# A hybrid decoder layer on one core: the low halves of weights kept in DRAM between two token halves, and new rates for gathered steps

## The chip, the cores and the metric

The kernel runs on one core of a Trainium2 chip. The metric is the device time of one execution in microseconds (us). Before the change it was 3117.79 us, the median of 3 runs (3115.04 to 3124.81 us).

The core's engines are TensorE (PE in the profile; its weight loads are PEld), VectorE (DVE), ScalarE (ACT), GpSimd (POOL) and SyncE (SP). SyncE and GpSimd issue DMA transfers from queues of their own, each strictly in order; the same holds for each engine's instructions.

## The reference, cut to what matters

One decoder layer over 1024 tokens of width 1024:

```
h    = rms_norm(x);  proj = h @ w_in                       # 28 blocks of 128 columns, and 8 gate columns
x   += concat(diff_attention(...), mlstm(...)) @ w_out
xb   = rms_norm(x);  q = xb @ w_query                      # 16 blocks of 128 columns
s    = q . sub_keys;  top-16 twice -> 16 experts a head, 8 heads: eidx, softmax weights g
u    = expert_u[eidx];  a = gelu(xb . u);  x += sum(g * a * expert_v[eidx])
x   += sigmoid(rms_norm(x) @ w_ple_gate) * (p @ w_ple_proj)
out  = rms_norm(x)
```

All of it is float32, and the output must have float32's accuracy.

## The kernel before

**Halves.** A float32 product is made from three products of a faster format (`mm3s`): each operand is split into a high half (rounded, made by ScalarE) and a low half (the rest, made by VectorE as operand minus high half). `weight()` (L190 to L198) does that for one 128x1024 block of weights: SyncE loads `wraw`, ScalarE writes `whi` (L195), VectorE writes `wlo` (L196). `wraw` has 3 buffers, `whi` and `wlo` have 2 each.

**Stages.** `front(0)` does everything up to the queries for tokens 0 to 511, `front(1)` the same for tokens 512 to 1023; each goes through the same 53 weight blocks: 29 of `w_in`, 8 of `w_out`, 16 of `w_query`. A projection takes 24 matmuls of 128x512: 16 with `whi`, then 8 with `wlo`. In the queries, each block's scores go to VectorE's top-16 instructions (L719 to L724). Then come `dense_up` and `dense_down`, which handle the last five of the eight tiles of 128 tokens by computing with all 16384 experts (128 steps each, with `thi` and `tlo` split as above), and `tail`, which does the rest for each tile in the order 4, 0, 5, 6, 7, 1, 3, 2.

**Gathered steps.** The first three tiles (0 to 2) use gathers instead. A step of `sparse()` is one gather of `ru` (a row of `expert_u` for each token, 512 KB, issued by GpSimd, L827) with VectorE's product and sum over it (L843), and one gather of `rv` with VectorE's update of `ya` (L861): 384 of each in all, in 400 steps, after 14 short steps that choose the experts. The steps run beside the other stages: `pump(x)` adds x to a debt, and whole steps are issued from it. `front(1)` adds `F_RATE[0]` for each of 29 input blocks, `F_RATE[2]` for each of 8 output blocks, `F_RATE[1]` for each of 11 query blocks; `dense_up` adds `UP_RATE[0]` in each of its first 40 steps and `UP_RATE[1]` in the other 88; `dense_down` adds `DOWN_RATE` in each of 128. What is left is issued in the tail, 8 steps at a time, and a tile among 0 to 2 is begun there only when its steps are done: its `ya` is stored to `x3_s` and loaded again as `x3`.

**Order.** A scheduler puts the instructions of each engine in one order before the run. Gathered steps have low priority, and VectorE's part of them may not stand ahead of the instruction last named by `anchor()`: in the fronts that is the last `wlo`.

**The chain at the end of a head.** `mlstm()` ends with `ry`, a reciprocal root in 13 tiny VectorE instructions (`rsqrt`, L118 to L127, and L556). ScalarE scales with it (L366), TensorE transposes the result (L561) and can only then go on with the last output block.

Of the kernel before, what the change touches and what calls it, by code (L numbers as in the profile page):

```python
# [8 lines left out]
F32 = mybir.dt.float32  # L9
F32R = mybir.dt.float32r  # L10
# [4 lines left out]
AF = mybir.ActivationFunctionType  # L15
# [4 lines left out]
P = 128  # L20
D = 1024
S = 1024
T = 512
NT = T // P
NPART = S // T
DC = D // P
H = 4
PH = 8
# [36 lines left out]
WR = 3  # L65
# [2 lines left out]
TORD = [4, 0, 5, 6, 7, 1, 3, 2]  # L68
TAIL_RATE = 8.0
TKEYS = [(0, q) for q in range(4)] + [(0, -1), (1, -1)] + [(1, q) for q in range(4)]  # L70
F_RATE = (1.8, 1.3, 1.5)
UP_RATE = (0.9, 1.45, 40)
QUIET = 5
DOWN_RATE = 1.05


@with_exitstack
def layer(ctx, tc, x, xT, pT, gcols, grows, win, convw, convb, gbias, lams, wout, wq, subk,
# [3 lines left out]
    def pool(name, bufs=1, **k):  # L82
        if k.get("space") != bass.MemoryType.DRAM:
            k["reuse_waits"] = "tile"
        return tc.tile_pool(name=name, bufs=bufs, **k)

    v, sc, pe, gp, sy = nc.vector, nc.scalar, nc.tensor, nc.gpsimd, nc.sync

    const = ctx.enter_context(pool("const", bufs=1))
    dram = ctx.enter_context(pool("dram", bufs=1, space=bass.MemoryType.DRAM))  # L90
# [14 lines left out]
    x2_s = dram.tile([S // P, P, D], F32, name="x2_s")  # L105
    h2_s = dram.tile([S // P, P, D], F32, name="h2_s")
    x3_s = dram.tile([S // P, P, D], F32, name="x3_s")
    g_s = dram.tile([P // GB * NDT, P, P, GB], F32, name="g_s")
    ga_s = dram.tile([P, P, TD], F32, name="ga_s")

# [76 lines left out]
            v.scalar_tensor_tensor(fcs["nlam"], le[:, 1:2], -LAM0, le[:, 0:1], op0=OP.add,  # L187
                                   op1=OP.subtract)

    def weight(wpool, src, shape):  # L190
        raw = wpool.tile([P, 1024], F32, name="wraw", bufs=WR)
        sy.dma_start(raw, src.rearrange("p a b -> p (a b)"))
        hi = wpool.tile([P] + shape, F32R, name="whi", bufs=2)
        lo = wpool.tile([P] + shape, F32R, name="wlo", bufs=2)
        sc.activation(hi.rearrange("p a b -> p (a b)"), raw, AF.Copy)  # L195
        anchor(v.tensor_sub(lo.rearrange("p a b -> p (a b)"), raw,  # L196
                            hi.rearrange("p a b -> p (a b)").bitcast(F32)))
        return hi, lo  # L198

    pumped = {"gen": None, "due": 0.0, "at": None}  # L200
# [1 line left out]
    def anchor(ins):  # L202
        pumped["at"] = ins.ins.name
# [16 lines left out]
    def front(part, ptk):  # L220
        t0 = part * NT
        with ExitStack() as c1:
            wp = c1.enter_context(pool(f"wp{part}", bufs=1))
            mmp = c1.enter_context(pool(f"mmp{part}", bufs=2, space=PSUM))
            sps = c1.enter_context(pool(f"sps{part}", bufs=2, space=PSUM))
            trp = c1.enter_context(pool(f"trp{part}", bufs=2, space=PSUM))
            with pool(f"pa{part}", bufs=1) as pa:
                hh = act.tile([P, DC, T], F32R, name="ahi")
                hl = act.tile([P, DC, T], F32R, name="alo")
                ready = {7 * H: weight(wp, win[7 * H], [DC, P])}  # L230
                for dc in range(DC):
                    if dc % 2 == 0:
                        x2t = pa.tile([P, 2, T], F32, name="p", bufs=3)
# [2 lines left out]
                    sc.activation(hh[:, dc, :], xt, AF.Copy, scale=gcol[:, GMIX + dc:GMIX + dc + 1])  # L236
                    xlo = v.scalar_tensor_tensor(hl[:, dc, :], xt, gcol[:, GMIX + dc:GMIX + dc + 1],  # L237
                                                 hh[:, dc, :].bitcast(F32), op0=OP.mult, op1=OP.subtract)
                ready[0] = weight(wp, win[0], [DC, P])
                anchor(xlo)  # L240
                if part == 0:
                    front_consts(fc)
# [46 lines left out]

                def project(blk):  # L290
                    pump(F_RATE[0] * part)
                    hi, lo = ready.pop(blk) if blk in ready else weight(wp, win[blk], [DC, P])
                    ps = mmp.tile([P, T], F32, name="mm")
                    mm3s([(ps, hi[:, dc, :], lo[:, dc, :], hh[:, dc, :], hl[:, dc, :], dc == 0, dc == DC - 1)
                          for dc in range(DC)], ("hr", "l"))
                    return ps
# [16 lines left out]
                lf = pa.tile([P, NT, H], F32, name="lf")  # L313
# [288 lines left out]

                def out_quarter(blk, q, first, last):
                    pump(F_RATE[2] * part)
                    hi, lo = weight(wp, wout[blk, q], [2, 512])
                    mm3s(sum([out_terms(blocks[blk], hi, lo, q, i, first, last) for i in range(NT)], []),
                         ("hl", "r"))

# [18 lines left out]
            with pool(f"pb{part}", bufs=1) as pb_:  # L627
# [19 lines left out]
                out_quarter(1, 0, True, False)  # L647
                out_quarter(1, 1, False, False)
                pump(2 * F_RATE[2] * part)
                lastq = [weight(wp, wout[1, q], [2, 512]) for q in (2, 3)]  # L650
                r2 = {}
                for i in range(NT):
                    mm3s(sum([out_terms(blocks[1], *lastq[q - 2], q, i, False, q == 3) for q in (2, 3)], []),
# [38 lines left out]
                pair = []  # L692
                for hc in range(2):
                    pump(F_RATE[1] * part)
                    pair.append((*weight(wp, wq[hc], [DC, P]), mmp.tile([P, T], F32, name="mm")))
                for cs in (slice(0, T // 2), slice(T // 2, T)):
                    for a in pair:
                        mm3s(query_terms(*a, cs), ("hl", "r"))
                for hc in range(2 * PH):
                    sk = pb_.tile([P, P], F32, name="sk", bufs=2)  # L700
                    sy.dma_start(sk, subk[hc])
                    if hc < 2:
                        ps = pair[hc][2]
                    else:
                        pump(F_RATE[1] * part if hc < 2 * PH - QUIET else 0)
                        hi, lo = weight(wp, wq[hc], [DC, P])
                        ps = mmp.tile([P, T], F32, name="mm")
                        mm3s(query_terms(hi, lo, ps, slice(0, T)), ("hr", "l"))
                    qq = pb_.tile([P, T], F32, name="qq", bufs=2)
# [234 lines left out]
    def dense_up(ptk):  # L944
        qh, ql = fcs["q"]
        chunks = [(qh, ql, 0, CH1)]
        with ExitStack() as c1:
# [29 lines left out]
            for j in range(P):  # L977
                pump(UP_RATE[0 if j < UP_RATE[2] else 1])
                hi, lo = head.pop() if head else table(dp, ut[j])
# [25 lines left out]
    def dense_down(yac):  # L1005
        with ExitStack() as c1:
# [30 lines left out]
            for g0 in range(0, P, GC):  # L1037
                pump(DOWN_RATE * GC)
                if g0 == FLUSH:
# [256 lines left out]
```

## Time and profile before

| | us |
|---|---|
| median of 3 runs | 3117.79 |
| the profiled execution, its own time | 3123.69 |
| its span, first to last instruction | 3121.9 |
| TensorE busy in it | 2873.4 |
| VectorE busy in it | 2557.4 |
| GpSimd busy in it | 1007.6 |

The stages in the profiled execution: `front(0)` 0 to 436 us, `front(1)` to 974, `dense_up` to about 2010, `dense_down` to about 2935, `tail` to the end; neighbours overlap a little.

How the rows below are read. In a row of windows stand the stretch and its length, then busy time (and number) of PE, PEld, DVE, ACT and POOL, the granted clock of TensorE (1.00 is 2.4 GHz), the busy share of the 16 DMA engines and GB/s. In a row of the timeline stand start, duration, engine, line, operation, output<-inputs, shape, number, and in brackets the engine's idle time before it and what ended it. In a group by line stand the count, then busy time and mean ns of one, then idle time before and its releasers. Busy matmuls are pipelined, so their durations overlap.

### The profile page before, as it was taken

Reading aid. Unit: us, or ns where it says so; the run is one execution under the profiler, and the core shown is the slowest. Engines: PE = TensorE matmul, PEld = TensorE weight load, DVE = VectorE, ACT = ScalarE, POOL = GpSimd, SP = SyncE. Lnnn points to the kernel's source line nnn. Section 1 sums busy time; section 2 is a strip of 40 time slices with the busy share of each in tenths; the row PEclk is TensorE's granted clock in tenths of the full one; section 3 lists DMA queues with packets and bytes.
Section 4 is the critical chain, followed back from the end, with each engine's and each line's share of the span. In section 5 each row is a group of like instructions: output and inputs, shape, how many; then the busy total and the mean of one; then the engine's idle time right before and its main releaser. Section 6 shows DMA issues by size and latency. Waiting matters only on the chain.

```text
span 3121.9 us, 44819 instructions
## 1 busy us (share of the span) xinstructions
PE 2873.4 (92%) x16367; PEld 2517.4 (81%) x16367; DVE 2557.4 (82%) x5349; ACT 1317.8 (42%) x2152; POOL 1007.6 (32%) x786
## 2 busy tenths in 40 slices
PE   7999989998697999999999999899989999998894
PEld 6887868776586999998889999778768888887773
DVE  5565889888799889799999797678778888888795
ACT  5664336655222222487776565212222222232241
POOL 0000000334414333444444555434333444414431
PEclk9999989999898999999999999899999999999997
DMA  5333433777846787899999989999989999988763
GB/s 168 100 111 127 150 126 93 233 229 244 303 133 233 264 276 244 306 345 340 343 340 346 370 328 367 372 348 340 313 291 330 339 333 329 338 295 276 259 222 124
DMA packets 316797, 829.01 MB, mean 266 GB/s; under 512 B 26144, under 2 KB 115104, under 8 KB 314016
## 3 DMA queue, kind: packets, MB, share of 16 engines
q0 software_dynamic: 112608, 410.04, 37.6%
q1 hardware_dynamic: 185536, 374.16, 34.9%
q10 hardware_dynamic: 18432, 41.95, 3.5%
q8 instruction: 128, 2.10, 0.3%
q14 instruction: 93, 0.76, 0.1%
HBM read 715.43 MB, written 102.24 MB: 262 GB/s over the span
## 4 chain that ended last, share of the span: by engine, by line
PE 55%; DVE 15%; DMA 12%; issue 12%; ACT 3%; POOL 2%; another core or an unknown queue 0%; SPq 0%; DVEq 0%; ACTq 0%; POOLq 0%
PE A L145 23%; PE mm L145 12%; PE keep L145 5%; DMA raw<-in_vr 4%; DMA rv<-in_ev,eidx 3%; DVE ya L861 3%; PE S L145 2%; DVE ru L843 2%; PE pg L931 2%; PE Y L136 2%; PE Y L137 2%; PE Y L138 2%; DVE tlo L881 1%; DMA ru<-in_eu,eidx 1%; POOL ru L827 1%
## 5 line engine op out<-in xcount | busy, mean ns | idle before, releaser
L827 POOL DMA_INDIRECT ru<-in_eu,eidx x384 | 508.4, 1324 | 1169.7 <-DVE ru L843 843.0
L827 POOL DMA_INDIRECT rv<-in_ev,eidx x384 | 491.2, 1279 | 443.5 <-DVE ya L861 286.8
L861 DVE SCALAR_TENSOR_TENSOR ya<-rv,cf,ya 128x1024 f32<-128x1024 f32 x384 | 492.3, 1282 | 46.5 <-DMA rv<-in_ev,eidx 29.3
L843 DVE SCALAR_TENSOR_TENSOR ru<-ru,sh 128x1024 f32<-128x1024 f32 x384 | 468.1, 1220 | 33.5 <-DMA ru<-in_eu,eidx 23.1
L881 DVE TENSOR_TENSOR tlo<-raw,thi 128x1024 fp32r<-128x1024 f32 x256 | 312.6, 1221 | 220.4 <-ACT thi L880 130.4
L880 ACT ACTIVATE thi<-raw 128x1024 fp32r<-128x1024 f32 x256 | 267.7, 1057 | 524.5 <-DMA raw<-in_vr 272.6
L145 PE MATMUL A<-ahi,thi 128*128 128x384 f32 x1024 | 348.7, 341 | 13.2 <-ACT thi L880 13.2
L145 PE MATMUL A<-alo,thi 128*128 128x384 f32 x1024 | 345.8, 338 | 0.0
L145 PE MATMUL mm<-ahi,whi 128*128 128x512 f32 (+1 forms) x752 | 301.4, 405 | 25.0 <-ACT ahi L236 13.1
L145 PE MATMUL mm<-alo,whi 128*128 128x512 f32 (+1 forms) x752 | 287.1, 394 | 7.1 <-DVE alo L237 7.1
L136 PE MATMUL Y<-thi,ph 128*128 128x512 f32 x640 | 250.2, 391 | 5.1 <-ACT thi L880 5.0
L145 PE MATMUL A<-xh,thi 128*128 128x256 f32 x1024 | 252.8, 284 | 0.7 <-ACT xh L971 0.7
L145 PE MATMUL A<-xl,thi 128*128 128x256 f32 x1024 | 252.7, 284 | 0.1
L137 PE MATMUL Y<-tlo,ph 128*128 128x512 f32 x640 | 250.0, 391 | 1.1 <-DVE tlo L881 1.0
L138 PE MATMUL Y<-thi,pl 128*128 128x512 f32 x640 | 249.4, 390 | 0.0
L1059 ACT ACTIVATE ph<-aq 128x640 fp32r<-128x640 f32 x128 | 87.3, 727 | 328.5 <-PE Y L137 309.4
L145 PEld LDWEIGHTS A<-ahi,thi 128*128 128x128 f32 x1024 | 193.6, 189 | 13.5 <-ACT thi L880 13.5
L145 PE MATMUL A<-ahi,tlo 128*128 128x384 f32 x1024 | 203.3, 337 | 0.0
L145 PE MATMUL keep<-tlo,ph 128*128 128x512 f32 x640 | 178.6, 403 | 22.7 <-DVE tlo L881 22.6
L145 PE MATMUL mm<-ahi,wlo 128*128 128x512 f32 (+1 forms) x752 | 193.9, 389 | 5.1 <-DVE wlo L196 5.0
L145 PEld LDWEIGHTS A<-xh,thi 128*128 128x128 f32 x1024 | 194.5, 190 | 1.0 <-ACT xh L971 0.9
L145 PEld LDWEIGHTS A<-xl,thi 128*128 128x128 f32 x1024 | 194.7, 190 | 0.3 <-DVE xl L972 0.3
(467 smaller groups left out, 6080.6 us busy)
## 6 DMA issues: line engine op xcount, KB each, us to landing
raw<-in_ut SPq DMA_DIRECT2D x128, 512.0 KB
raw<-in_vr SPq DMA_DIRECT2D x128, 512.0 KB
ga_s<-ga ACTq DMA_DIRECT2D x128, 320.0 KB
g_s<-st SPq DMA_DIRECT2D x20, 2048.0 KB
gq<-g_s SPq DMA_DIRECT2D x32, 1280.0 KB
aq<-ga_s SPq DMA_DIRECT2D x32, 1280.0 KB
wraw<-in_win SPq DMA_DIRECT2D x58, 512.0 KB
wraw<-in_wq SPq DMA_DIRECT2D x32, 512.0 KB
```

Source lines behind the costliest of these rows:

```text
L136: pe.matmul(o, lh, rh, start=start, stop=False)
L137: pe.matmul(o, lh, rl, start=False, stop=False)
L138: pe.matmul(o, ll, rh, start=False, stop=stop)
L145: pe.matmul(o, ll if p == "l" else lh, rl if p == "r" else rh, start=start and p == "h", stop=stop and n == last and p == names[-1])
L827: gp.indirect_dma_start(out=b, out_offset=None, in_=table, in_offset=bass.IndirectOffsetOnAxis(ap=eidx[part][:, i, k:k + 1], axis=0))
L843: behind(v.scalar_tensor_tensor(b, b, 1.0, st["h", tl], op0=OP.mult, op1=OP.mult, accum_out=st["d", n][:, j:j + 1]))
L861: op = v.scalar_tensor_tensor(ya, b, st["c", n][:, j:j + 1], ya, op0=OP.mult, op1=OP.add)
L880: sc.activation(hi, raw, AF.Copy)
L881: anchor(v.tensor_sub(lo, raw, hi.bitcast(F32)))
L931: pe.matmul(pg[:, b, :], o0[:, 4 * a + b, :], wc[:, c, a % 2, b, :], start=c == 0, stop=c == 1)
L1059: sc.activation(ph, av, AF.Copy)
```

## The change

`front(0)` still computes each `wlo`, and GpSimd then writes it to a DRAM buffer `lo_s`, one slot for each of the 53 blocks. In `front(1)` `wlo` is not computed: SyncE loads it from `lo_s`, right behind `wraw`. There `wraw` has 2 buffers instead of 3, and `wlo` has 3 instead of 2. The anchor of the gathered steps moves: in `front(1)` it is ScalarE's `whi`, in `front(0)` `weight()` sets none. Three rates rise: `F_RATE[0]` from 1.8 to 1.9, `UP_RATE[0]` from 0.9 to 1.2, `DOWN_RATE` from 1.05 to 1.1.

```diff
-F_RATE = (1.8, 1.3, 1.5)
-UP_RATE = (0.9, 1.45, 40)
+F_RATE = (1.9, 1.3, 1.5)
+UP_RATE = (1.2, 1.45, 40)
...
-DOWN_RATE = 1.05
+DOWN_RATE = 1.1
...
+    lo_s = dram.tile([7 * H + 9 + 2 * PH, P, D], F32, name="lo_s")
...
-    def weight(wpool, src, shape):
-        raw = wpool.tile([P, 1024], F32, name="wraw", bufs=WR)
+    def weight(wpool, src, shape, part, n):
+        raw = wpool.tile([P, 1024], F32, name="wraw", bufs=WR - part)
         sy.dma_start(raw, src.rearrange("p a b -> p (a b)"))
         hi = wpool.tile([P] + shape, F32R, name="whi", bufs=2)
-        lo = wpool.tile([P] + shape, F32R, name="wlo", bufs=2)
-        sc.activation(hi.rearrange("p a b -> p (a b)"), raw, AF.Copy)
-        anchor(v.tensor_sub(lo.rearrange("p a b -> p (a b)"), raw,
-                            hi.rearrange("p a b -> p (a b)").bitcast(F32)))
+        lo = wpool.tile([P] + shape, F32R, name="wlo", bufs=2 + part)
+        hf, lf = (a.rearrange("p a b -> p (a b)") for a in (hi, lo))
+        if part:
+            sy.dma_start(lf.bitcast(F32), lo_s[n])
+            anchor(sc.activation(hf, raw, AF.Copy))
+        else:
+            sc.activation(hf, raw, AF.Copy)
+            v.tensor_sub(lf, raw, hf.bitcast(F32))
+            gp.dma_start(lo_s[n], lf.bitcast(F32))
         return hi, lo
...
-                ready = {7 * H: weight(wp, win[7 * H], [DC, P])}
+                ready = {7 * H: weight(wp, win[7 * H], [DC, P], part, 7 * H)}
...
-                    hi, lo = weight(wp, wout[blk, q], [2, 512])
+                    hi, lo = weight(wp, wout[blk, q], [2, 512], part, 7 * H + 1 + 4 * blk + q)
...
-                        hi, lo = weight(wp, wq[hc], [DC, P])
+                        hi, lo = weight(wp, wq[hc], [DC, P], part, 7 * H + 9 + hc)
```

Line numbers after the change are 1 higher from L108 on and 6 higher behind `weight()`.

Where it moves instructions. VectorE in `front(1)`, in the `ry` chain of the last head; before, from the fourth instruction of the chain (`ru` and `ya` are gathered steps):

```order
L120 TENSOR_SCALAR ry_u_7748<-ry_i_7747 128x4
L843 SCALAR_TENSOR_TENSOR ru_7574,dots_7222<-ru_7574,sh2_5346 128x1024
L125 TENSOR_TENSOR ry_h_7749<-ry_u_7748 128x4
L861 SCALAR_TENSOR_TENSOR ya_6281<-rv_7577,cf_7219,ya_6281 128x1024
L126 TENSOR_TENSOR ry_h_7749<-ry_h_7749,ry_m_7746 128x4
L843 SCALAR_TENSOR_TENSOR ru_7662,dots_7222<-ru_7662,sh2_5346 128x1024
L127 SCALAR_TENSOR_TENSOR ry_u_7748<-ry_h_7749,ry_u_7748 128x4
L861 SCALAR_TENSOR_TENSOR ya_6281<-rv_7665,cf_7219,ya_6281 128x1024
```

After, from just ahead of the third:

```order
L867 SCALAR_TENSOR_TENSOR ya_6220<-rv_8001,cf_7994,ya_6220 128x1024
L120 TENSOR_SCALAR ry_i_7819<-ry_m_7818 128x4
L849 SCALAR_TENSOR_TENSOR ru_8004,dots_7997<-ru_8004,sh2_5284 128x1024
L121 TENSOR_SCALAR ry_u_7820<-ry_i_7819 128x4
L867 SCALAR_TENSOR_TENSOR ya_6220<-rv_8007,cf_7994,ya_6220 128x1024
L126 TENSOR_TENSOR ry_h_7821<-ry_u_7820 128x4
L127 TENSOR_TENSOR ry_h_7821<-ry_h_7821,ry_m_7818 128x4
L128 SCALAR_TENSOR_TENSOR ry_u_7820<-ry_h_7821,ry_u_7820 128x4
```

Before, 12 instructions of gathered steps stand between the chain's first instruction and L556, one after nearly each link; now 3 do, and from the fifth link on the chain is unbroken.

ScalarE at the end of `front(1)`; `cf` belongs to the gathered steps and needs all of a unit's 16 `ru`, `thi` is the high half of `dense_up`'s first block. Before:

```order
L710 ACTIVATE qq_9264<-mm_9239 128x512
L726 ACTIVATE sif1_8174<-si_9205 128x4x16
L726 ACTIVATE sif1_8174<-si_9271 128x4x16
L710 ACTIVATE qq_9330<-mm_9305 128x512
L850 ACTIVATE cf_9397<-dots_7973 128x16
L880 ACTIVATE thi_9392<-raw_9388 128x1024
L880 ACTIVATE thi_9508<-raw_9507 128x1024
```

After:

```order
L732 ACTIVATE sif1_8246<-si_9215 128x4x16
L716 ACTIVATE qq_9340<-mm_9315 128x512
L732 ACTIVATE sif1_8246<-si_9281 128x4x16
L716 ACTIVATE qq_9406<-mm_9381 128x512
L732 ACTIVATE sif1_8246<-si_9347 128x4x16
L886 ACTIVATE thi_9468<-raw_9464 128x1024
L886 ACTIVATE thi_9580<-raw_9579 128x1024
```

`cf` no longer stands ahead of the first `thi`; it has gone to an earlier place among the queries.

VectorE in the queries of `front(0)`, at the `wlo` of the eleventh of the 16 blocks. Before, 20 rows of the top-16 stand between it and the next block's:

```order
L724 MAX_INDEX si_3831<-sv0_3213,wk_3844 128x8
L721 MATCH_REPLACE wk_3850<-sv0_3213,tr_3826 128x128
L196 TENSOR_TENSOR wlo_3928<-wraw_3925,whi_3927 128x1024
L723 MAX sv0_3213<-wk_3850 128x8
L719 MAX sv0_3213<-tr_3892 128x8
L724 MAX_INDEX si_3831<-sv0_3213,wk_3850 128x8
```

After, between those of the tenth and the twelfth:

```order
L727 MATCH_REPLACE wk_3897<-sv0_3251,tr_3873 128x128
L202 TENSOR_TENSOR wlo_3909<-wraw_3906,whi_3908 128x1024
L729 MAX sv0_3251<-wk_3897 128x8
L202 TENSOR_TENSOR wlo_3976<-wraw_3973,whi_3975 128x1024
L730 MAX_INDEX si_3878<-sv0_3251,wk_3897 128x8
L202 TENSOR_TENSOR wlo_4043<-wraw_4040,whi_4042 128x1024
L725 MAX sv0_3251<-tr_3940 128x8
```

Three `wlo` now stand nearly side by side; such threes occur twice in the queries of `front(0)` before and four times after. The third of a three takes the buffer of the first.

## Rows read from the trace of the kernel before

**Rows 1.** Windows, one row for each stage; columns in the order of the engines.
```profile
0.00:436.00 436.00, 406.00 (x2137) 334.44 (x2137) 285.58 (x1051) 226.08 (x512) 3.04 (x9) 0.98 0.39 127
436.00:974.00 538.00, 453.07 (x2391) 372.24 (x2391) 475.29 (x1491) 250.03 (x537) 146.06 (x121) 0.92 0.62 204
974.00:1300.00 326.00, 322.29 (x2186) 320.53 (x2187) 287.32 (x866) 95.07 (x153) 122.87 (x94) 0.99 0.79 274
1300.00:2010.00 710.00, 674.08 (x5274) 658.37 (x5273) 618.64 (x638) 474.59 (x581) 333.23 (x249) 1.00 0.93 345
2010.00:2935.00 925.00, 887.93 (x3822) 728.28 (x3821) 752.50 (x960) 216.12 (x268) 345.48 (x265) 0.97 0.92 318
2935.00:3122.00 187.00, 130.00 (x562) 103.60 (x560) 138.12 (x349) 55.87 (x108) 56.92 (x48) 0.85 0.59 193
```

**Rows 2.** Timeline, TensorE, second front: waits; in brackets idle time and releaser.
```profile
792.70 1.35 PE L561 MATMUL tr<-ident,t 128*128 128x128 f32 x4 [24.11 <-ACT t L366]
...
876.37 3.03 PE L145 MATMUL mm<-ahi,wlo 128*128 128x512 f32 x12 [1.69 <-DVE wlo L196]
...
954.27 3.78 PE L145 MATMUL mm<-ahi,wlo 128*128 128x512 f32 x8 [3.29 <-DVE wlo L196]
...
974.10 0.69 PE L145 MATMUL A<-ahi,thi 128*128 128x384 f32 x1 [13.23 <-ACT thi L880]
```

**Rows 3.** Timeline, VectorE, the last `ry` chain: first and last.
```profile
768.90 0.17 DVE L118 TENSOR_SCALAR ry_m<-yss 128x4 f32<-128x4 f32 x1
...
792.06 0.15 DVE L556 TENSOR_TENSOR ry_u<-ry_u,den 128x4 f32<-128x4 f32 x1
```

**Rows 4.** Timeline, ScalarE, end of the second front.
```profile
972.89 0.22 ACT L850 ACTIVATE cf<-dots 128x16 f32<-128x16 f32 x1 [14.14 <-DVE ru L843]
973.01 1.99 ACT L880 ACTIVATE thi<-raw 128x1024 fp32r<-128x1024 f32 x2
```

**Rows 5.** Groups by line, VectorE, second front: the halves' subtraction.
```profile
L196 DVE TENSOR_TENSOR wlo<-wraw,whi 128x1024 fp32r<-128x1024 f32 x53 | 64.4, 1215 | 8.5 <-ACT whi L195 4.6 <-issue 2.5 <-PE mm L145 0.6
```

**Rows 6.** Groups by line, VectorE, tail: gathered steps.
```profile
L861 DVE SCALAR_TENSOR_TENSOR ya<-rv,cf,ya 128x1024 f32<-128x1024 f32 x34 | 43.5, 1281 | 15.8 <-DMA rv<-in_ev,eidx 15.7
...
L843 DVE SCALAR_TENSOR_TENSOR ru<-ru,sh 128x1024 f32<-128x1024 f32 x18 | 21.9, 1218 | 5.3 <-DMA ru<-in_eu,eidx 5.3
```

**Rows 7.** Timeline, VectorE, first queries: three subtractions close together.
```profile
354.12 1.21 DVE L196 TENSOR_TENSOR wlo<-wraw,whi 128x1024 fp32r<-128x1024 f32 x1
...
355.46 1.20 DVE L196 TENSOR_TENSOR wlo<-wraw,whi 128x1024 fp32r<-128x1024 f32 x1
...
357.60 1.23 DVE L196 TENSOR_TENSOR wlo<-wraw,whi 128x1024 fp32r<-128x1024 f32 x1 [0.66 <-ACT sif L726]
...
359.38 0.30 DVE L719 MAX8 sv<-tr 128x8 f32<-128x128 f32 x1 [0.56 <-PE tr L713]
```

**Rows 8.** Timeline, SyncE: stores of `x2` issued.
```profile
307.71 6.18 SPq L665 DMA_DIRECT2D x_s<-x  x3
```

**Rows 9.** Timeline, GpSimd: a load that waited for that store.
```profile
312.46 0.70 POOL L858 DMA_DIRECT2D ya<-x_s  x1 [312.00 <-DMA x_s<-x]
```

**Rows 10.** Timeline, TensorE, start of the second front.
```profile
443.10 0.79 PE L145 MATMUL mm<-alo,whi 128*128 128x512 f32 x1 [7.13 <-DVE alo L237]
```

**Rows 11.** Timeline, VectorE, just before it.
```profile
439.64 1.20 DVE L196 TENSOR_TENSOR wlo<-wraw,whi 128x1024 fp32r<-128x1024 f32 x1
...
442.30 1.41 DVE L237 SCALAR_TENSOR_TENSOR alo<-p,gcol,ahi 128x512 fp32r<-128x512 f32 x2
```

**Rows 12.** Groups by line, VectorE, first part of the dense up stage.
```profile
L881 DVE TENSOR_TENSOR tlo<-raw,thi 128x1024 fp32r<-128x1024 f32 x47 | 57.3, 1220 | 33.8 <-issue 33.8
```

**Rows 13.** Timeline, TensorE, the tail's last tile.
```profile
3093.98 1.97 PE L1139 MATMUL tr<-ident,x 128*128 128x128 f32 x8 [34.00 <-DMA x<-x_s]
```

**Rows 14.** Timeline, SyncE, the tail's end.
```profile
3088.09 0.33 SPq L865 DMA_DIRECT2D x_s<-ya  x1
...
3118.04 1.00 SPq L1183 DMA_DIRECT2D out_dram<-x  x2
```

More of the change, by code (lines that the diff above doesn't have):

```diff
@@ L238, in front @@
                                                  hh[:, dc, :].bitcast(F32), op0=OP.mult, op1=OP.subtract)
-                ready[0] = weight(wp, win[0], [DC, P])
+                ready[0] = weight(wp, win[0], [DC, P], part, 0)
                 anchor(xlo)
@@ L291, in project @@
                     pump(F_RATE[0] * part)
-                    hi, lo = ready.pop(blk) if blk in ready else weight(wp, win[blk], [DC, P])
+                    hi, lo = ready.pop(blk) if blk in ready else weight(wp, win[blk], [DC, P], part, blk)
                     ps = mmp.tile([P, T], F32, name="mm")
@@ L649, in front @@
                 pump(2 * F_RATE[2] * part)
-                lastq = [weight(wp, wout[1, q], [2, 512]) for q in (2, 3)]
+                lastq = [weight(wp, wout[1, q], [2, 512], part, 7 * H + 5 + q) for q in (2, 3)]
                 r2 = {}
@@ L694, in front @@
                     pump(F_RATE[1] * part)
-                    pair.append((*weight(wp, wq[hc], [DC, P]), mmp.tile([P, T], F32, name="mm")))
+                    pair.append((*weight(wp, wq[hc], [DC, P], part, 7 * H + 9 + hc), mmp.tile([P, T], F32, name="mm")))
                 for cs in (slice(0, T // 2), slice(T // 2, T)):
```

## The prediction, made before the changed kernel ran

> **What bounds the kernel now.** I read the windows by stage first [rows 1]. TensorE is busy 406 of 436 us in the first front, 322 of 326 in the first part of `dense_up`, 674 of 710 in the rest of it and 888 of 925 in `dense_down`: there only TensorE's work counts, and work moved to another engine is free while that engine has room. Two stages are different. In the second front TensorE is idle for 538 − 453.1 = 84.9 us, while VectorE is busy 475.3 of 538, 88%. In the last 187 us TensorE is idle for 57 us.
>
> Then I read what TensorE waits for in these two. In the second front [rows 2] the longest wait is 24.1 us for ScalarE's scaling by `ry`; at the end there are 13.2 us for `thi`, and two waits for a `wlo`, 1.7 and 3.3 us; at its start stand 7.1 us for `alo` [rows 10]. That leaves 84.9 − 24.1 − 13.2 − 5.0 − 7.1 = 35.5 us in small pieces. In the tail one wait holds most of the idle time: 34.0 us for `x3` of the last tile [rows 13]. SyncE stores the last `ya` at 3088.09 us, TensorE goes on at 3093.98, and the output leaves at 3118.04 [rows 14]. So the end hangs on the last gathered step, and VectorE's part of those is 34 + 18 = 52 instructions in the tail, 21.0 us of idle time before them spent on their gathers [rows 6].
>
> **Tail: −34 us.** The higher rates move steps forward: 0.1 × 29 = 2.9 in the second front, 0.3 × 40 = 12 in `dense_up`, 0.05 × 128 = 6.4 in `dense_down`, together 21.3 steps, or 43 instructions of VectorE (each step has a `ru` and a `ya`). Of 52 about 9 stay; I count 13, as the last lag behind their gathers. Their pace before was (3088 − 2935) / 52 = 2.9 us each, so they end near 2935 + 13 × 2.9 = 2973. TensorE would come to the last tile at 3093.98 − 34.00 = 3059.98, 87 us later: cover for 29 more of them. The wait goes whole, and the rest runs as before. What is late next is TensorE's own work for the tile, perhaps a few us of it closer to the other tiles' vector work: −30 to −38.
>
> **Second front: −42 us**, in five pieces.
> The `ry` chain takes from 768.90 to 792.06, 23.2 us, for 13 instructions of about 0.15 us [rows 3]; nearly all of it is the 12 gathered instructions between its links, 1.2 to 1.3 us each and some waiting for a gather. In the new order 3 stand there, and none behind the fifth link: 3 × 1.3 + 13 × 0.17 = 6.1, say 6.4. Gain 17; from 5, if gathered work delays the chain's input instead, to 19.
> The two waits for `wlo` go, as nothing is computed there: −5.
> At the end, ScalarE's `cf` stood ahead of the first `thi` and waited 14.14 us for VectorE's `ru` [rows 4]; now it has gone among the queries. The 13.2 us of TensorE become about 2, the time of one `thi`: −11 (0 if `thi` finds another wait, its own load say).
> At the start, two subtractions of 1.20 us go from VectorE ahead of `alo` [rows 11], but GpSimd's loads of `xT` now stand in its queue behind all 53 writes of halves, the last of which can be issued only some us before that: net −1, between −3 and +10.
> The remaining 35.5 us of idle time: VectorE loses 53 subtractions, 64.4 us [rows 5], and gets 2.9 steps, 6 instructions of 1.25 us, 8 us. It falls from 475 busy us to about 419. Where VectorE is what TensorE waits for in small pieces, they shrink; I take −8, between 0 and −25.
> Beside it, 53 halves are read, 53 × 0.524 MB = 27.8 MB. The 16 DMA engines moved 204 GB/s at a share of 0.62 there [rows 1], 329 GB/s when full, so this is 84 us and a share of 0.78. SyncE's loads are in order, the half right behind its `wraw`; three `wlo` buffers let it start about two blocks, 2 × 538 / 53 = 20 us, before it is used. I cost it at nothing; if that cover is gone, each of 53 waits counts (rival C).
>
> **First front: +8 us.** The subtractions stay, and 53 writes are added, which GpSimd issues; it was busy 3 of 436 us. At 0.70 us an issue, as its load in [rows 9], they take 37 us of it. 27.8 MB at 127 / 0.39 = 326 GB/s take the DMA share from 0.39 to 0.59. What counts is that a `wlo` buffer is free only when its write has ended. Normally it comes round after two blocks, 2 × 436 / 53 = 16 us, which hides it. In the queries, where three subtractions stand together, the third takes the buffer of the first; it starts 2.27 us after the first ends (355.33 to 357.60) [rows 7]. The trace has no such write; the nearest is the first of the three stores of `x2`, 512 KB too, issued at 307.71 [rows 8]; GpSimd's load of that tile waited for it until 312.46 [rows 9]: 4.75 us. So VectorE, with the top-16 behind the subtraction, stands for 4.75 − 2.27 = 2.5 us; 0.56 us behind the third it waited for TensorE's transposes anyway. That is 1.9 us, four times in the new order: 8 us. Below it is bounded by 0 (the write lands in 2.27 us, or waits behind it absorb all), above by twice the duration, 4 × (9.5 − 2.8) = 27. For a single write the Trainium skill ("DMA: Bandwidth & Descriptors", Anatomy of one DMA — SWDGE (gpsimd) path) gives about 2.0 us and bytes / 436 000 per us. That would be an estimate of 3.2 us and a stall of 0.4 us after the cover, so 1 to 2 us for four and a total 6 us better; I keep to the row, since its 4.75 us were seen here.
>
> **`dense_up`: +5 us.** 12 steps are 24 instructions of 1.25 us, 30 us of VectorE in the first 326 us, where it has 326 − 287.3 = 38.7 us free, 33.8 of them ahead of `tlo`, waiting for nothing that the profile shows [rows 12]. It just fits, but `tlo` now and then stands behind a gathered instruction, and TensorE has only 3.7 us of slack. 0 to 31: all of it, if none fits. Its 24 gathers, 12.6 MB, fit beside a share of 0.79.
>
> **`dense_down`: +5 us.** 13 more instructions take 16 us of the 172 that VectorE has free. The 12.8 gathers are 6.7 MB; at 318 GB/s that is 21 us of transfers in a stage whose share is 0.92 [rows 1]. I take a quarter, 5, between 0 and 21. The Trainium skill speaks against me here: "DMA: Bandwidth & Descriptors", Issuing engines are not separate DMA queues, says that transfers of all engines interleave on the same 16 DMA engines, so gathers push back the streamed weights. No row shows it doing so (TensorE is busy 96% at that share); by it alone `dense_down` would cost 21 and the sum be 16 us worse, which is part of rival A.
>
> **The sum** is −34 − 42 + 8 + 5 + 5 = −58 us. The profiled execution took 3123.7 us of its own (span 3121.9), so 3066 after; from the median 3117.8, 6 us lower, it is 3060.
>
> **Rivals.**
> A, the moved steps are paid back in the dense stages: 31 instead of 5 in `dense_up`, 15 instead of 5 in `dense_down`, +36: 3096. For it speaks that DMA stands at 0.92 to 0.93 there and TensorE at 95% or more; against it that VectorE has 38.7 and 172 us free, and that one stage's late gather doesn't stop TensorE.
> B, the writes of halves are slow, 10 us instead of 4.75, and VectorE stalls 7.2 us at each of four places, 29 instead of 8: 3081. For it: the queries read and write at once; against: a share of only about 0.59.
> D, the rest of TensorE's idle time in the second front goes too, 25 us more, as VectorE falls from 88% to 78%: 3035. Against it: much of this time follows ScalarE and chains of small steps, not a full VectorE.
> C, slower: the halves come late in the second front. SyncE is in order, so a half whose buffer is still in use holds back the next `wraw`, which has a buffer less, and each block makes TensorE wait. From 58 / 53 = 1.1 us a block on, nothing of the gain is left; at 2 us it is +106: 3166. A whole transfer may take 4.75 us, so 2 isn't far off; against it stand 20 us of lead and a share of 0.78.
>
> **How the numbers follow.** Forecast 60% (its own range 3040 to 3080), A 16%, B 10%, D 9%, C 5%. The range 3030 to 3100 takes in D, B and A, and leaves out C and the far ends of the others. A measurement tells about 0.3%, 9.4 us, from no change: 3108.4 is the border, which only C and the worst part of A pass. Faster 0.92, same 0.03, slower 0.05.
>
> **What would show it.** Tail: no wait of TensorE for `x3` of the last tile, and the last `ya` stored over 80 us before TensorE begins that tile. Second front: less than 10 us of idle time at the transpose behind `ry`; no `cf` ahead of the first `thi`; VectorE near 419 us; waits for `wlo` now name a DMA, and are few. First front: its end 5 to 10 us later, with stalls of 2 to 3 us at the third `wlo` of each three, released by a write. `dense_up`'s first 326 us at most 5 us longer with 24 more gathered instructions, `dense_down` likewise. I am wrong if TensorE waits for `wlo` by the dozen (C), if the dense stages grow by more than 20 us (A), or if the wait in the tail moves to another tile instead of going.

## The result, and the profile after

The changed kernel takes 3087.9 us (median of 4 runs, 3083.68 to 3091.56) against 3118.5 us of the kernel before beside it: a ratio of 0.9896 with a 95% interval of 0.9879 to 0.9913. So it is about 1% faster. The forecast said 3060 with a range of 3030 to 3100: the direction and the range held, the gain is 31 us instead of 58.

The windows of the profiled execution after (own time 3091.56 us, span 3089.8), in the columns of [rows 1]:

```profile
0.00:436.00 436.00, 398.78 (x2087) 327.49 (x2088) 269.84 (x955) 220.53 (x502) 29.18 (x58) 0.97 0.56 181
436.00:974.00 538.00, 475.74 (x2443) 389.69 (x2441) 433.77 (x1508) 254.23 (x542) 151.48 (x132) 0.92 0.78 271
974.00:1300.00 326.00, 317.76 (x2142) 315.78 (x2142) 312.48 (x932) 93.95 (x151) 153.97 (x117) 0.99 0.84 303
1300.00:2010.00 710.00, 678.84 (x5315) 663.34 (x5315) 623.11 (x645) 476.49 (x582) 341.53 (x249) 1.00 0.93 347
2010.00:2935.00 925.00, 886.32 (x3818) 724.11 (x3818) 763.90 (x971) 217.87 (x272) 359.99 (x275) 0.98 0.93 323
2935.00:3090.00 155.00, 130.85 (x568) 104.91 (x566) 97.29 (x292) 54.68 (x104) 12.65 (x11) 0.92 0.30 102
```

Against [rows 1], VectorE fell in the second window by 41.5 us (56 forecast), and the DMA share rose from 0.62 to 0.78, the share that was worked out. Fixed windows hide where time was lost, though, since the work shifts through them. So I took the start of the same TensorE instruction in the two timelines. In the tail and at the ends of the second front the forecast's waits are gone. TensorE's timeline after; these answer to [rows 2] and [rows 13]:

```profile
817.27 1.35 PE L567 MATMUL tr<-ident,t 128*128 128x128 f32 x4 [3.51 <-ACT t L372]
...
976.04 0.54 PE L146 MATMUL A<-ahi,thi 128*128 128x384 f32 x1 [2.36 <-ACT thi L886]
...
3062.00 1.03 PE L1145 MATMUL tr<-ident,x 128*128 128x128 f32 x8
```

The wait behind the last `ry` is 3.5 us instead of 24.1, that for the first `thi` 2.4 instead of 13.2, and the last tile waits for nothing instead of 34.0. The `ry` chain on VectorE, first and last link, and SyncE's store of the last `ya` (compare [rows 3] and [rows 14]):

```profile
810.97 0.17 DVE L119 TENSOR_SCALAR ry_m<-yss 128x4 f32<-128x4 f32 x1 [1.06 <-ACT jb L559]
...
816.62 0.16 DVE L562 TENSOR_TENSOR ry_u<-ry_u,den 128x4 f32<-128x4 f32 x1
```

```profile
2983.46 0.33 SPq L871 DMA_DIRECT2D x_s<-ya  x1
```

The chain takes 5.7 us (6.4 forecast), and the last store comes 78.5 us before TensorE begins the last tile.

What the forecast did not see stands ahead of these. The next rows are windows of equal work, cut at the same TensorE instructions to within a few us: first the middle of the second front, then the stretch with the last `ry`. Before:

```profile
521.00:754.00 233.00, 217.38 (x1222) 181.00 (x1221) 203.88 (x470) 145.73 (x343) 70.28 (x58) 0.98 0.67 216
754.00:793.00 39.00, 14.89 (x84) 12.32 (x82) 28.80 (x53) 7.84 (x22) 19.62 (x17) 0.74 0.89 329
```

After:

```profile
539.00:799.00 260.00, 228.66 (x1219) 188.74 (x1218) 200.71 (x459) 146.01 (x345) 97.00 (x83) 0.92 0.84 288
799.00:818.00 19.00, 15.49 (x86) 12.81 (x84) 13.25 (x34) 9.35 (x23) 8.21 (x7) 0.94 0.91 328
```

The stretch with `ry` gained 20 us, but the middle lost 27. TensorE's idle time rose there by 15.7 us (from 15.6 to 31.3), and the same matmuls took 11.3 us more, at a granted clock of 0.92 instead of 0.98. VectorE is as busy as before (200.7 against 203.9), although 23 subtractions of 1.2 us are gone: 25 more gathered instructions had come in. GpSimd is busier by 27 us, with 83 issues instead of 58: gathers that stood later before.

The following table is worked out from the timelines: by how many us the same TensorE instruction starts later (+) or earlier in each run than in the kernel before (at 768.6, how much later its idle time ahead of 792.7 begins). Two runs whose fronts have the same code (rates 1.5) differ by 5.6 us at the start of `dense_up`, so differences below about 6 us mean nothing.

| start before, and where | after | rates | halves | no reads | no writes | late | 1.5 / 1.2 | 1.5 / 1.1 |
|---|---|---|---|---|---|---|---|---|
| 467.7 second front, its first blocks | +17.4 | −1.1 | +16.0 | +18.6 | −1.4 | +16.5 | −3.8 | −2.0 |
| 557.0 scores | +33.4 | −1.0 | +32.7 | +31.2 | +11.3 | +20.4 | −3.1 | −2.4 |
| 737.7 last head | +37.2 | −1.6 | +30.7 | +26.4 | +7.8 | +34.8 | −10.4 | −5.6 |
| 768.6 where the wait behind `ry` begins | +45.2 | −1.6 | +35.3 | +32.4 | +14.9 | +37.4 | −6.3 | −3.3 |
| 792.7 behind `ry` | +24.6 | −2.0 | +15.7 | +12.8 | −4.7 | +38.2 | −21.7 | −18.7 |
| 850.4 first queries | +16.7 | +1.5 | +6.5 | +3.6 | −14.1 | +29.3 | −22.2 | −16.8 |
| 1038.6 `dense_up`, begun | +6.2 | +6.3 | −5.1 | −6.5 | −23.9 | +20.9 | −25.6 | −20.0 |
| 1944.8 `dense_up`, near its end | −0.7 | +1.3 | −3.2 | −12.3 | −30.9 | +15.3 | −29.8 | −25.0 |
| 3094.0 last tile | −32.0 | −30.2 | −10.3 | −43.1 | −63.5 | −12.3 | −42.7 | −45.2 |

The first column is the result by stages; the others are experiments that follow (the last two, with the rates 1.5 and 1.2 or 1.1, have no halves in DRAM).

### The profile page after: what moved, and what is told of

It reads as the page before. It is cut to its first block, busy times and chain, and to the rows that moved or that the text cites. A ratio compares the mean times of both kernels' runs of the same rounds, so it can differ in the third digit from the quotient of the medians.

```text
span 3089.8 us, 44968 instructions
## 1 busy us (share of the span) xinstructions
PE 2888.3 (93%) x16367; PEld 2525.3 (82%) x16367; DVE 2500.4 (81%) x5296; ACT 1317.8 (43%) x2152; POOL 1048.8 (34%) x839
## 4 chain that ended last, share of the span: by engine, by line
PE 49%; DVE 16%; issue 14%; DMA 13%; ACT 5%; POOL 2%; SPq 0%; DVEq 0%; ACTq 0%; POOLq 0%
PE A L146 22%; PE mm L146 9%; DMA raw<-in_vr 6%; DVE ya L867 4%; PE acc L146 3%; PE keep L146 3%; PE S L146 2%; DVE aq L1064 2%; DVE tlo L887 2%; DMA rv<-in_ev,eidx 2%; DVE ru L849 2%; PE pg L937 2%; DMA dd<-qk 2%; DVE yac L1085 1%; ACT st L940 1%
## 5 line engine op out<-in xcount | busy, mean ns | idle before, releaser
L833 POOL DMA_INDIRECT rv<-in_ev,eidx x384 | 508.3, 1324 | 492.7 <-DVE ya L867 293.7
L867 DVE SCALAR_TENSOR_TENSOR ya<-rv,cf,ya 128x1024 f32<-128x1024 f32 x384 | 491.7, 1280 | 36.8 <-DMA rv<-in_ev,eidx 24.8
L146 PE MATMUL A<-ahi,tlo 128*128 128x384 f32 x1024 | 203.9, 337 | 1.2 <-DVE tlo L887 1.2
L146 PEld LDWEIGHTS A<-alo,thi 128*128 128x128 f32 x1024 | 194.1, 190 | 0.0
```

The lines of the kernel that those rows point to most:

```text
L146: pe.matmul(o, ll if p == "l" else lh, rl if p == "r" else rh, start=start and p == "h", stop=stop and n == last and p == names[-1])
L833: gp.indirect_dma_start(out=b, out_offset=None, in_=table, in_offset=bass.IndirectOffsetOnAxis(ap=eidx[part][:, i, k:k + 1], axis=0))
L867: op = v.scalar_tensor_tensor(ya, b, st["c", n][:, j:j + 1], ya, op0=OP.mult, op1=OP.add)
```

## The experiments

**Which half of the change brings the time?** Four runs: the new rates alone, the halves alone, the halves without their reads, and the anchor alone.

Rates alone, in the kernel before:

```diff
-F_RATE = (1.8, 1.3, 1.5)
-UP_RATE = (0.9, 1.45, 40)
-DOWN_RATE = 1.05
+F_RATE = (1.9, 1.3, 1.5)
+UP_RATE = (1.2, 1.45, 40)
+DOWN_RATE = 1.1
```

> The kernel before with the three new rates and nothing else; the halves are computed twice as before. The question behind all four runs: the changed kernel lost 27 us between 485 and 785 us, in the middle of the second front, where I had forecast a gain of 8. Theory T (transfers): the 53 reads of halves delay the small round trips through DRAM and the gathers there. Rival G (gathered steps): the steps stand earlier there, because the anchor went to ScalarE and the first rate rose. Both: the wait of 34 us in the tail goes. T: the second front is at most 5 us longer (6 more gathered instructions), total about 3088. G, if the rate is its cause: 10 to 20 us longer there, total 3098 to 3105.

Measured: 3090.6 us, ratio 0.9904 (0.9889 to 0.9919). This is the whole gain. The wait in the tail is gone, and the second front is within 2 us of before up to `ry`; `dense_up` begins 6 us later.

Halves alone, the changed kernel with the old three rates (the same lines, the other way round):

> The changed kernel with the three old rates: halves are written and read back, the anchor is on ScalarE. Both: the wait in the tail is back, about 33 us. T: the loss in the middle of the second front stays at 20 us or more, total about 3118 to 3121, no better than before. G, if the rate is its cause: the loss falls to 10 us or less, total about 3103 to 3108.

Measured: 3118.6 us, ratio 0.9993 (0.9983 to 1.0002): no change. The loss in the middle is there (+16.0 to +30.7), so the rate is not its cause. `dense_up` begins 5 us earlier than before.

Only three halves read:

```diff
-        lo = wpool.tile([P] + shape, F32R, name="wlo", bufs=2 + part)
...
         if part:
-            sy.dma_start(lf.bitcast(F32), lo_s[n])
+            if n not in kept and len(kept) < 3:
+                kept[n] = wpool.tile([P, 1024], F32R, name=f"wlo{len(kept)}")
+                sy.dma_start(kept[n].bitcast(F32), lo_s[n])
+            lo = list(kept.values())[n % len(kept)].rearrange("p (a b) -> p a b", a=shape[0])
```

> The changed kernel with only three of the 53 halves read back, once, into buffers that stay; every block of the second front uses one of these three, so its products with low halves are not the reference's. Writes, anchor and rates as in the changed kernel. T: the loss of 27 us in the middle of the second front goes to 5 or less, and the loads of xT are as late as before; total about 3088 - 25 = 3063. G: the loss stays, total 3083 to 3088.

Measured: 3081.1 us, ratio 0.9877 (0.9861 to 0.9892), some 6 us less than the changed kernel, at the edge of what can be told. In the profile `dense_up` begins 13 us earlier. Between 467.7 and 737.7 the loss is 8 us instead of 20, but most of the jump at 557.0 is there (12.0 us from 540 on, against 15.0 in the changed kernel). So both theories were half right: the reads cost something like 10 us in the second front, and most of the jump is not theirs.

The anchor alone, in the kernel before:

```diff
-        sc.activation(hi.rearrange("p a b -> p (a b)"), raw, AF.Copy)
-        anchor(v.tensor_sub(lo.rearrange("p a b -> p (a b)"), raw,
-                            hi.rearrange("p a b -> p (a b)").bitcast(F32)))
+        anchor(sc.activation(hi.rearrange("p a b -> p (a b)"), raw, AF.Copy))
+        v.tensor_sub(lo.rearrange("p a b -> p (a b)"), raw,
+                     hi.rearrange("p a b -> p (a b)").bitcast(F32))
```

> The kernel before with the anchor of the gathered steps moved from VectorE's subtraction to ScalarE's high half, in both fronts, and nothing else. T: the same time as before, 3118 within 6 us. G, if the anchor is its cause: the steps begin some 20 us earlier in the second front, which gets 15 to 25 us longer; total 3133 to 3143.

Measured: 3124.3 us, ratio 1.0013 (1.0001 to 1.0025), and 46 gathered instructions begun by the last head, as before. With the halves it is 71 at the new rates and 66 at the old. With the new rates alone it is 46 too. So the steps stand earlier once the subtractions are gone; neither the anchor alone nor the rate moves them. VectorE's order has room, and the scheduler fills it with gathered steps.

**Where do the halves lose?** The jump at 557.0 in the changed kernel, in the chain of waits (start, duration, what):

```profile
551.28 0.08 DVE ru L849
551.36 0.60 DVE qk L379
...
553.90 10.13 DMA dd<-qk
...
564.11 0.64 ACT qab L283
```

A gathered `ru` stands on VectorE ahead of `qk`; `qk` goes through DRAM and comes back as `dd`, 10.1 us later, and TensorE waits for it. In the kernel before no gather was under way at this place: its first is issued at 551.5, behind these transfers; in the changed kernel the first is issued at 545.5, ahead of them. To test it I issued the first steps later.

```diff
-                    pump(F_RATE[0] * part)
+                    blks[0] += part
+                    pump(F_RATE[0] * 29 / 22 * part if blks[0] > 7 else 0)
```

> The changed kernel with no steps issued in the first 7 of the 29 input blocks of the second front, and 29/22 of the rate in the other 22, so that the same number is issued by the end of the input blocks. On VectorE the first gathered instruction then stands three blocks later, where it stood in the kernel before. Theory P (place): the jump of 15 us between 540 and 560 us comes from gathered instructions that stand ahead of the head's small steps there; it goes, and the second front ends 8 to 15 us earlier, total 3073 to 3080. Rival D (bytes): the jump is the reads' and stays, total 3085 to 3090.

Measured: 3109.9 us, ratio 0.9956 (0.9942 to 0.9971): 22 us slower than the changed kernel. The jump did go (+16.5, then +20.4), as the theory said, and the total did not follow. The steps now crowd behind it: between the starts 737.7 and 792.7 of the table VectorE begins 25 gathered instructions, as in the kernel before, and 13 in the changed kernel. So the wait behind `ry` is back. TensorE, and the windows of the middle and of the stretch with `ry`:

```profile
830.87 1.35 PE L570 MATMUL tr<-ident,t 128*128 128x128 f32 x4 [24.84 <-ACT t L375]
```

```profile
541.00:790.00 249.00, 225.37 (x1210) 186.30 (x1209) 201.97 (x496) 145.08 (x340) 85.31 (x71) 0.92 0.78 269
790.00:832.00 42.00, 17.16 (x92) 13.98 (x90) 28.21 (x58) 10.52 (x26) 21.26 (x19) 0.75 1.01 386
```

So the short `ry` chain of the changed kernel is no gift of the halves as such: its gathered steps had gone to the middle. What they cost there the two runs with fewer transfers tell: from 467.7 to 768.6 the loss is 28 us in the changed kernel, 14 without the reads and 16 with neither reads nor writes, and all three gain 20 to 21 behind `ry`.

Theory P named VectorE's order, but the run tells only that the steps are the cause. The chain above shows how: the gathered `ru` takes under 1 us of it, the transfer of `dd` 10.1. The loads of `dd` (from `qk` and `kt_s`) at the head before, where no gather is under way, land in 2.2 to 3.0 us (median 2.3), with the reads of halves beside them; those issued from 552.0 to 577.1 take 4.8 to 10.1 (median 8.5). With neither reads nor writes it is 2.2 to 2.8 and then 3.6 to 8.6. In the kernel with the rates 1.5 and 1.1, which has no halves in DRAM, it is 2.2 to 3.8 (median 2.5) ahead of the first gather, and 2.4 to 6.9 (median 5.9) at the next head, where gathers are under way. So `dd` is slow where gathers move beside it: some 8 of its 10.1 us, more than VectorE's order costs. Of the 15 us of the jump, 7.6 are idle time of TensorE, the rest goes with its lower granted clock (0.79 from 558.4 to 590.4, 1.00 for the same work before).

The reads on another queue:

```diff
-            sy.dma_start(lf.bitcast(F32), lo_s[n])
+            sc.dma_start(lf.bitcast(F32), lo_s[n])
```

> The changed kernel with the loads of halves issued by ScalarE's queue instead of SyncE's. Reads cost about 11 us in the second front (its end with three halves read once was 13 us earlier). Theory Q (queue): they hold up the small round trips behind them on SyncE's queue; on another queue this goes, total 3076 to 3080. Rival D (bytes): the bytes themselves delay what else is under way, total 3085 to 3090. ScalarE's instructions behind a load that waits for its buffer could make it slower than 3090.

Measured: 3100.1 us, ratio 0.9922 (0.9908 to 0.9936), slower than the changed kernel by 12 us. The second front is the same (`dense_up` begins at +5.5, against +6.2), so SyncE's queue is not what costs; ScalarE's waits for `dd<-qk` in the second front add up to 42.6 us, against 36.8 in the changed kernel, 30.3 without the reads, 33.0 with neither reads nor writes and 15.1 before. So most of the rise comes with the earlier gathers, not with the halves' transfers. Why the dense stages are longer in this run is open.

Another buffer for the first front:

```diff
-        raw = wpool.tile([P, 1024], F32, name="wraw", bufs=WR - part)
+        raw = wpool.tile([P, 1024], F32, name="wraw", bufs=WR - 1)
-        lo = wpool.tile([P] + shape, F32R, name="wlo", bufs=2 + part)
+        lo = wpool.tile([P] + shape, F32R, name="wlo", bufs=3)
```

> The changed kernel with two wraw and three wlo buffers in the first front too. The rates alone gave the whole gain, and the halves nothing, so I ask what the halves cost. The first front got 14 us longer: 6 in its first 70 us, 8 in the queries. Theory B (buffer): the third subtraction of three waits for the write of the first, so with a third buffer the 8 us in the queries go, total about 3080. Rival W (writes): the transfers themselves slow the loads of weights, a third buffer changes nothing, total 3088; with only two wraw even a few us more.

Measured: 3089.4 us, ratio 0.9887 (0.987 to 0.9904): no difference, so theory B was wrong. The stall that I forecast is in the changed kernel as told, at the third of each three. VectorE's timeline there:

```profile
367.03 1.23 DVE L202 TENSOR_TENSOR wlo<-wraw,whi 128x1024 fp32r<-128x1024 f32 x1 [3.88 <-DMA lo_s<-wlo]
...
388.79 1.22 DVE L202 TENSOR_TENSOR wlo<-wraw,whi 128x1024 fp32r<-128x1024 f32 x1 [3.91 <-DMA lo_s<-wlo]
...
410.58 1.22 DVE L202 TENSOR_TENSOR wlo<-wraw,whi 128x1024 fp32r<-128x1024 f32 x1 [3.93 <-DMA lo_s<-wlo]
...
432.45 1.22 DVE L202 TENSOR_TENSOR wlo<-wraw,whi 128x1024 fp32r<-128x1024 f32 x1 [4.03 <-DMA lo_s<-wlo]
```

With the third buffer these four waits go, but the scheduler now puts the subtractions in pairs, 40 rows of the top-16 apart, and TensorE and VectorE wait for each other once a pair. TensorE and VectorE of that run:

```profile
417.10 3.04 PE L146 MATMUL mm<-ahi,wlo 128*128 128x512 f32 x12 [0.90 <-DVE wlo L202]
```

```profile
421.16 0.30 DVE L725 MAX8 sv<-tr 128x8 f32<-128x128 f32 x1 [2.51 <-PE tr L719]
```

Two blocks take 14.57 us (417.10 to 431.67, where the next such wait stands), three in the changed kernel 21.8 (388.79 to 410.58): 7.3 us a block either way. So the time does not hang on these waits alone; that the order in which the subtractions stand costs it is likely, but not shown by itself.

Without the writes, too:

```diff
-            gp.dma_start(lo_s[n], lf.bitcast(F32))
+            if n in (28, 0, 1):
+                gp.dma_start(lo_s[n], lf.bitcast(F32))
```

> The run with three halves read once, and now only those three written as well; the other 50 are not written, so the second front's low products are again not the reference's. Order, anchor and rates as in the changed kernel. Theory W (writes): the 14 us that the first front loses, 6 at its start and 8 in the queries, and the late loads of xT, come from the writes; they go, total 3063 to 3070 against 3081 with the writes. Rival O (order): they come from where VectorE's subtractions stand in the new order; total 3077 to 3083.

Measured: 3059.9 us, ratio 0.9801 (0.9783 to 0.982), 21 us less than with the writes (0.9877), as far as theory W reached or a little farther. The second front begins 1.4 us earlier than before instead of 18.6 later. One thing in the expectation was not so: the order changed with the writes. VectorE's subtractions in the later queries stand some 20 rows apart again, but for one pair, as in the kernel before; with the writes they stand in threes. So the 21 us are the transfers and what the scheduler makes of them; this run doesn't part the two. The second front still has 69 gathered instructions begun by the last head.

**Can the rates do it alone?** If a gathered instruction costs its full time in the second front, fewer steps there should help without any halves. Four runs, three of them the kernel before with other rates:

```diff
-F_RATE = (1.8, 1.3, 1.5)
-UP_RATE = (0.9, 1.45, 40)
-DOWN_RATE = 1.05
+F_RATE = (1.5, 1.3, 1.5)
+UP_RATE = (1.2, 1.55, 40)
+DOWN_RATE = 1.2
```

> The kernel before, without any of the halves' transfers, with F_RATE[0] 1.5, UP_RATE 1.2 and 1.55, DOWN_RATE 1.2: 8.7 steps fewer in the second front than before, 12 more in the first part of dense_up, 8.8 more in its second part, 19 more in dense_down. Theory V (VectorE bounds the second front, the dense stages take steps for almost nothing): against the three new rates alone (3090.6) the second front is 10 to 20 us shorter, the dense stages at most 8 longer, total 3075 to 3085. Rival A (paid back): TensorE waits for streamed weights in the dense stages, total 3092 to 3100.

Measured: 3081.7 us, ratio 0.9871 (0.9855 to 0.9888). At TensorE's first instruction of `dense_up` (974.1 before) 85 gathered instructions have begun instead of 112, and it comes 35.9 us earlier, 10 of these by the wait for `thi`: 26 us for 27 instructions, about 1 us each. By 1038.6 it is 116 instead of 130, and 25.6 us are left. But the first to the last of `dense_down`'s products with `tlo` now take 938.5 us instead of 905.8: at this rate that stage does not take steps for nothing, and rival A is half right.

With `F_RATE[0]` 1.4, `UP_RATE` 1.2 and 1.6, `DOWN_RATE` 1.1:

> The kernel before, no halves in DRAM, with F_RATE[0] 1.4, UP_RATE 1.2 and 1.6, DOWN_RATE 1.1. Against F_RATE[0] 1.5, UP_RATE 1.2 and 1.55, DOWN_RATE 1.2, which gave 3081.7 and lost about 31 us in dense_down: 4 fewer instructions in the second front, 8 more in the rest of dense_up, 26 fewer in dense_down. Theory (a gathered instruction costs its full 1.25 us in the second front and nothing in dense_up and in dense_down up to a rate of 1.1): second front 5 shorter, dense_down 20 to 30 shorter, total 3052 to 3060. Rival (the rest of dense_up is full at 1.55): it gets 10 to 15 longer, total 3065 to 3075.

Measured: 3078.9 us, ratio 0.9864 (0.9848 to 0.988). `dense_down` gave its time back (900.5 us), but between 1038.6 and 1944.8 the run lost 17 us where the one with 1.55 gained 4. So the rest of `dense_up` is full at about 1.55. Its second front was not shorter, either: it reaches 1038.6 at −18.0, the run with 1.5 at −25.6. The expected 3052 to 3060 was wrong; the rival's size was right for the stage.

The same rates in the changed kernel, halves and all:

> The changed kernel, halves and all, with the same rates as the run with F_RATE[0] 1.4. Theory N (the halves' gain and price cancel whatever the rates): the same time as that run within 6 us. Rival V (the halves help as VectorE bounds the second front; with 24 fewer gathered instructions there it no longer does): the price stays and the gain shrinks, 10 to 20 us slower than that run. If instead the halves and fewer steps add up, it is 5 to 10 us faster.

Measured: 3081.8 us, ratio 0.9871 (0.9853 to 0.989): the same as without halves, within the intervals. The halves bring nothing at these rates either. Between 1038.6 and 1944.8 this run loses 14.5 us, so the rate of 1.6 is too high with halves as well.

`F_RATE[0]` 1.5, `UP_RATE` 1.2 and 1.55, `DOWN_RATE` 1.1, in the kernel before:

> The kernel before, no halves in DRAM, with F_RATE[0] 1.5, UP_RATE 1.2 and 1.55 and DOWN_RATE 1.1: the fronts and dense_up of the run with 1.55 (30 us ahead of before when dense_up ended) and the dense_down of the runs with 1.1 (0 to 5 us longer than before). If the stages are independent, the terms add: -30, +3, and -33 to -37 for the wait in the tail, 3056 to 3062. Rival: the stages are linked, and steps that dense_down no longer takes are late in the tail or shift the load elsewhere; 3070 to 3082, as the two runs that it is made of.

Measured: 3075.5 us, ratio 0.9849 (0.9835 to 0.9862). It is the fastest kernel with the whole computation here, and its interval lies below that of the changed kernel. The terms did not add, though: 25.0 us ahead near the end of `dense_up`, it is only 11.0 ahead at 2949.5, in the tail. `dense_down` took 918.1 us, where the run without writes took 908 with the same rate in it. What made it longer is open.

## Why the prediction came out right in range and wrong in size

The profiled executions differ by 32.1 us (3123.7 to 3091.6), and the table's first column parts them. That the range held is owed to the tail's term, which is the rates' own: of the 34 us that the forecast gave the two fronts together (−42 and +8) none is left where `dense_up` has begun (+6.2).

- **Tail, −34.** Right: from 2949.5, where the two runs are 0.5 us apart, to the last tile it is −32.5. The wait went whole and no other took its place, as the cover of 87 us was 78.5.
- **`ry`, −17; `wlo`, −5; `thi`, −11.** Right: −20.6 at the wait behind `ry` (from +45.2 to +24.6), −11.1 for `thi` (from +13.0 where its wait begins to +1.9), less 4.3 that small waits behind it took back (for `xl`, 3.86 us instead of 1.51). Between the two it is −11.6 instead of −5: the waits for `wlo` went, and so did part of others (4.32 us for VectorE's `x` at 806.88 became 0.44).
- **First front, +8, and the start of the second, −1.** The mechanism was right in part and the size too small: +17.4 for 7. The stall stands at the four places named, 3.9 us each on VectorE where 2.5 were forecast: the write frees its buffer 5.5 us after the first subtraction instead of 4.75, and the third stands 1.6 us behind the first instead of 2.27. TensorE loses 8 us there, the forecast's figure, but partly by luck: with a third buffer the stall goes and a block takes as long. The other parts were missed: 6 us in the first 70 us (TensorE waits 9.17 us for a `whi` instead of 7.44, 1.42 us for a `kab`, and the granted clock falls for a stretch behind it), and 3.5 us at the start of the second front, where a three's last subtraction kept TensorE waiting 4.97 us. Without the writes all this goes.
- **The rest of the second front, −8.** This is the step that failed: from 467.7 to the wait behind `ry` it measured +28 (from +17.4 to +45.2). "VectorE loses 53 subtractions, 64.4 us, and gets 2.9 steps, 8 us" counted the whole front, and took the freed time to be slack for TensorE. But the scheduler filled it: 25 more gathered instructions by the last head, of which the rate accounts for 5 (66 instead of 71 at the old rates). About 14 of the 28 us go without the reads, the next term; the other 14 to 16 stay without reads and writes, nearly the 20 that `ry` gained. So the gain of `ry` and this part of the loss are the same steps seen at two places, and the forecast counted the gain alone.
- **Reads, 0.** Wrong by about 7 us in the times (3081.1 without them) and 13 in the second front's profile. Rival C's mechanism did not happen: the only wait of TensorE there that names a late half is one of 1.03 us for a weight load, 0.60 us for its matmul. The Trainium skill ("DMA: Bandwidth & Descriptors", Issuing engines are not separate DMA queues) fits the run on ScalarE's queue, where the same bytes cost the second front as much as on SyncE's.
- **`dense_up`, +5, `dense_down`, +5.** Both cost less: −5.6 and about 0. Rival A did not happen at rates of 1.2 and 1.1. Its part in `dense_down` did at a `DOWN_RATE` of 1.2: 938.5 us against 918.1 at 1.1, with the other rates alike.
- **Writes, price.** The 4.75 us of [rows 8] and [rows 9] were a good price: the page of the profile after gives a median of 5.1 us, and the writes took from 2.9 to 8.7. The Trainium skill's fit ("DMA: Bandwidth & Descriptors", Anatomy of one DMA — SWDGE (gpsimd) path), 3.2 us as an estimate, lies near the quickest of them and does not agree with the median.

```profile
lo_s<-wlo POOLq DMA_DIRECT2D x53, 512.0 KB, 5.1
```

By the runs, the halves without their transfers take 31 us off the rates' 3090.6, and with them 3. The run without the 50 writes and reads comes to 3059.9 us; the 28 us that are missing in the changed kernel are the price of the transfers, 21 for the writes with their order and 7 for the reads, of which the forecast had 8. That 3059.9 is the forecast's 3060 is a coincidence: in that run, too, the second front loses 16 us ahead of `ry`, where a gain of 8 was forecast, and `dense_up` gains 7, where a cost of 5 was. The gain of the change is that of the rates.

## What to carry to other kernels

Before you count a freed engine's time as a gain, ask who fills it: where a scheduler has low-priority work in hand, it moves that work into the hole, and a stall that you see vanish may have gone to a place that you don't look at. When a change has two parts, price each alone; here three numbers gave the whole gain, and the larger edit nothing. A wait at the very end, with nothing queued behind it, was the surest term of the sum. A small transfer that TensorE's work hangs on belongs into the sum too, if gathers move beside it.

## What was not expected of the hardware

The stretch in the middle lost 11.3 of its 27 us not by waiting but by slower matmuls: TensorE was busy 228.7 us for work that had taken 217.4, as the granted clock was 0.92 instead of 0.98. More short waits had come into this stretch: behind one of 2.68 us, at 563.49, matmuls took 0.63 us instead of 0.39, the lower of the clock's two levels (1.2 GHz instead of 2.4). By the mean clock, an estimate, 41 of the 260 us passed at the lower level, instead of some 10 of 233. A forecast by idle time alone misses that part. In `dense_up` a step more or less had hardly a price up to a rate of 1.55 (two runs gained 4 and 5 us between 1038.6 and 1944.8), and its full price or more at 1.6 (two runs lost 17 and 15, though their first rate differs too); `dense_down` took 900.5 to 918.1 us in the runs with 1.1, and 938.5 with 1.2.
